# Second token blocks of a mixture of experts put behind a branch on every engine, and a new spread of the weight splits

## Chip, cores and metric

The kernel runs on one core of one Trainium2 chip. The metric is the device time of one execution in microseconds (us). The engines are TensorE (PE; its weight loads are PEld), VectorE (DVE), ScalarE (ACT), GpSimd (POOL) and SyncE (SP), which issues most transfers.

## The reference

One layer over 2048 tokens of width 1024: adaLN-modulated RMSNorm, a combined projection, softmax attention and retention, an output projection with a gated residual, and then a hierarchical mixture of experts. The change lies in the last part alone. Each token goes to 2 of 32 experts, so that an expert has 128 tokens on average, and some have more:

```
def expert_block(args):
    x_blk, e = args
    return (jax.nn.silu(x_blk @ w_gate[e]) * (x_blk @ w_up[e])) @ w_down[e]
```

The weights of an expert are 1024x512 (gate), 1024x512 (up) and 512x1024 (down) in float32. The result of a token is the weighted sum over its two experts, times a gate (gt2), added to the residual stream, and a final RMSNorm follows.

## The kernel before

The expert part is the function moe_static, run under a manual schedule: each engine executes its instructions in the order in which the code writes them. One pass of its loop over s is called a stage here; there are 31 of them, and the last expert is written out behind the loop.

The first 128 tokens of an expert are its first block (b = 0), tokens 129 to 256 its second block (b = 1). An expert of over 128 tokens is called heavy here, the others light. More than 256 tokens are handled by moe_more behind the loop.

Stage s does the gate and up products of expert s (gu, 24 matmuls of 512 columns each), the down product of expert d = s - 1 (down, twice 12 matmuls), and gathers, transposes and splits the tokens of expert s + 1 (gather, xT). Every float32 operand is split into a high part (a copy on ScalarE) and a low part (a subtraction on VectorE), and a product is three passes over the parts.

The weights of an expert come as 12 tiles of 128x1024 (wraw), loaded by SP into 9 buffers. advance(k) splits the next k tiles into whi (17 buffers, line 1535) and wlo (15 buffers, line 1536). The tuple AD says how many tiles are split at each of ten places of a stage, 12 in all: adv(0) behind gu(s, 0), adv(1) behind gu(s, 1), adv(2) behind act(s, 0), adv(3) behind xT(s + 1, 0), adv(4) behind act(s, 1), adv(5) to adv(8) around the two halves of down, adv(9) at the end. The split of a tile into a reused wlo buffer has to wait until TensorE has used the old tile, in the second block's product too.

The matmuls of the second block (gu_part, down_part) and its gather and scatter are issued by more: it loads the expert's token count into a register of the engine and branches on it. All else of the second block is done for all 32 experts, with zeros where there are no tokens: the eight transposes and two splits of xT(e, 1); the two folds of act(e, 1) (line 1606 on ScalarE, line 1607 on VectorE; a fold adds the upper 64 rows onto the lower), its SiLU and its product; the four transposes and the split of hT(e, 1); the two folds of evac_part; and its two multiplications by gt2 on GpSimd (line 1630). TR is a pair of PSUM tiles (tr) that all transposes share, so a transpose has to wait until the one before is split.

A branch under the framework has a second arm: where the body is skipped, the engine waits until its own earlier instructions have ended and then counts its semaphore up by what the body would have. That wait is called a join here.

Of the kernel before, what the change touches and what calls it, by code (L numbers as in the profile page):

```python
# [2 lines left out]

# [1 line left out]

# [6 lines left out]
F32 = mybir.dt.float32  # L12
# [3 lines left out]
AF = mybir.ActivationFunctionType  # L16
ALU = mybir.AluOpType
# [4 lines left out]
P = 128  # L22
D = 1024
KD = D // P
L = 2048
# [30 lines left out]
WA = 8  # L56
EA, EB, FIN = 3, 1, (4, 10, NT)
A0, A1, A2 = 6, 2, 4
AD = (3, 5, 0, 0, 0, 0, 0, 2, 2, 0)
XT = 2  # L60
PC = (4, 2, 4, 2, 2, 4, 4, 4, 4, 2)
PS = (4, 2, 2, 0, 0, 0, 0, 0, 0, 0, 2, 2, 2, 0, 2, 0, 2, 0)
# [70 lines left out]
class Build:  # L133
# [1374 lines left out]
    def moe_static(self, p, ps):  # L1508
        nc, tc, a = self.nc, self.tc, self.a
# [3 lines left out]
        Y = [ps.tile([P, 512], F32, name=f"Y{n}") for n in range(2)]  # L1513
        TR = [ps.tile([P, 4, P], F32, name=f"tr{i}") for i in range(2)]
        XG = [p.tile([P, D], F32, name=f"xg{b}", bufs=1) for b in range(2)]
        W, XT, SG, HT = {}, {}, {}, {}
        loads = self.moe_loads
        raws = self.moe_raws
        order = self.moe_order
# [8 lines left out]
        def advance(k):  # L1528

            for n in range(split_at[0], min(split_at[0] + k, len(order))):  # L1530
                raw = raws.pop(0)
                e, i = order[n]
                hi = p.tile([P, 1024], F32R, name="whi", bufs=WBH)
                lo = p.tile([P, 1024], F32R, name="wlo", bufs=WBL)
                nc.scalar.copy(hi, raw)  # L1535
                nc.vector.tensor_sub(lo, raw, hi)  # L1536
                W[e, i] = hi, lo
                load(1)
                split_at[0] = n + 1
# [6 lines left out]
        def gather(e):  # L1546
            nc.gpsimd.indirect_dma_start(
                out=XG[0], out_offset=None, in_=self.h2_d,
                in_offset=bass.IndirectOffsetOnAxis(ap=self.slots[:, 2 * e, 0:1], axis=0), bounds_check=L - 1, oob_is_err=False)

        def gather_part(e, b):
# [2 lines left out]
                out=XG[1][at], out_offset=None, in_=self.h2_d,  # L1554
                in_offset=bass.IndirectOffsetOnAxis(ap=self.slots[at, 2 * e + 1, 0:1], axis=0), bounds_check=L - 1, oob_is_err=False)

        def xT(e, b):
            x = p.tile([P, KD, 2, P], F32R, name="xT", bufs=2)
            cols = XG[b].rearrange("t (i p k) -> t i k p", p=P, k=2)
            for half in range(2):  # L1560
                for i in range(4):
                    nc.tensor.transpose(TR[half][:, i, :], cols[:, 2 * half + i // 2, i % 2, :], self.ident)
            for half in range(2):
                s_ = slice(4 * half, 4 * half + 4)
                split(x[:, s_], TR[half], b)
            XT[e, b] = x

        def split(out, t, b):

            hi, lo = out[:, :, 0, :], out[:, :, 1, :]  # L1570
            if b:
                hi, lo = (o.rearrange("p k (n h) -> p k h n", h=2) for o in (hi, lo))
                t = t.rearrange("p k (h n) -> p k h n", h=2)
            nc.scalar.copy(hi, t)  # L1574
            nc.vector.tensor_sub(lo, t, hi)

        def product(out, l, e, m, cols, K, rows):

# [7 lines left out]
        def gu(e, m):  # L1586
            product(GU[:, m, :], XT[e, 0], e, m, slice(0, 512), KD, 1)
# [5 lines left out]
        def act(e, b):  # L1593
            G = (GU, GB)[b]
            sg = p.tile([P, DE], F32, name="sg", bufs=2)
            if b:
                up = p.tile([P, DE], F32, name="up", bufs=1)
                fold(e, G[:, 0, :], 0, sg)
                fold(e, G[:, 1, :], 1, up)
            nc.scalar.activation(sg, sg if b else G[:, 0, :], AF.Silu)  # L1600
            nc.vector.scalar_tensor_tensor(sg, sg, W1[:, e:e + 1] if b else self.slots[:, 2 * e, 1:2].bitcast(F32), up if b else G[:, 1, :], op0=ALU.mult, op1=ALU.mult)
            SG[e, b] = sg

        def fold(e, src, n, out):

            nc.scalar.activation(LOW[n][0:64], src[64:128], AF.Copy, scale=self.few[64:128, e:e + 1])
            nc.vector.tensor_add(out, src, LOW[n])

        def hT(e, b):
            sg = SG.pop((e, b))  # L1610
            h = p.tile([P, 4, 2, P], F32R, name="hT", bufs=2)
            for i in range(4):
                nc.tensor.transpose(TR[b][:, i, :], sg[:, i * P:(i + 1) * P], self.ident)
            split(h, TR[b], b)
            HT[e, b] = h

        def down(e, n):
            product(Y[n], HT[e, 0], e, 2, slice(n * 512, (n + 1) * 512), 4, 1)
# [6 lines left out]
            nc.vector.tensor_mul(y[:, n, :], Y[n], self.gt2[:, n * 512:(n + 1) * 512])  # L1625

        def evac_part(e, y):
            for n in range(2):
                fold(e, Y[n], n, y[:, n, :])
                nc.gpsimd.tensor_mul(y[:, n, :], y[:, n, :], self.gt2[:, n * 512:(n + 1) * 512])  # L1630

        def y_tile():
            return p.tile([P, 2, 512], F32, name="y", bufs=YB)
# [6 lines left out]
        def scatter(e, b, y):  # L1640
            at = slice(0, 64 * b + 64)
            nc.gpsimd.indirect_dma_start(
                out=self.acc_d, out_offset=bass.IndirectOffsetOnAxis(ap=S1[at, e:e + 1], axis=0),
                in_=y[at].rearrange("p n f -> p (n f)"), in_offset=None, compute_op=ALU.add, bounds_check=L - 1, oob_is_err=False)

        def more(eng, e, f, *args):

            n = eng.value_load(self.cnt[0:1, e:e + 1], min_val=0, max_val=L)
            with tc.If(n > P):
                with tc.If(n <= P + 64) as few:  # L1650
                    f(e, 0, *args)
                with few.Else():
                    f(e, 1, *args)
# [9 lines left out]
        LOW = [p.tile([P, 512], F32, name=f"low{n}", bufs=1) for n in range(2)]  # L1663
# [18 lines left out]
        W1 = p.tile([P, NE], F32, name="W1", bufs=1)  # L1682
        S1 = p.tile([P, NE], I32, name="S1", bufs=1)
        t = p.tile([P, 2, NE], F32, name="pick", tag="sg", bufs=2)
# [62 lines left out]
        def last_add(b, y):  # L1747
            nc.gpsimd.tensor_add(fin[NT + b], fin[NT + b], y.rearrange("p n f -> p (n f)"))
# [6 lines left out]
        def adv(i):  # L1755
            if s < NE - 2 or i < 7:
                advance(AD[i] if s else max(0, min(AD[i], sum(AD[:i + 1]) - A2)))

# [7 lines left out]
        def down_more(d):  # L1766
            more(nc.tensor, d, down_part)
            y = y_tile()
            evac_part(d, y)
            return y  # L1770

        for s in range(NE - 1):
            d = s - 1
            gu(s, 0)
            adv(0)
            if s == 1 and HE:
                for b in range(2):
                    hT(0, b)
            gu(s, 1)
            adv(1)  # L1780
            act(s, 0)
            adv(2)
            if s == NE - 2:
                advance(EB)
            else:
                xT(s + 1, 0)
                gather(s + 2)
            adv(3)
            more(nc.tensor, s, gu_part)
            act(s, 1)  # L1790
            adv(4)
            if d >= 0:
                y = y_tile()
                down(d, 0)
                evac(0, y)
            adv(5)
            if s < NE - 2:
                xT(s + 1, 1)
            if s + 2 < NE:
                more(nc.gpsimd, s + 2, gather_part)  # L1800
            adv(6)
            if d >= 0:
                down(d, 1)
                evac(1, y)
                scatter_all(d, y)
                adv(7)
                y = down_more(d)
                adv(8)
                more(nc.gpsimd, d, scatter, y)
            else:  # L1810
                adv(7)
                adv(8)
            if s or not HE:
                hT(s, 0)
                hT(s, 1)
            adv(9)
            if s == NE - 2:
                advance(EA)
                fin["g"] = p.tile([P, D], F32, name="whi", bufs=WBH)
                nc.sync.dma_start(fin["g"], self.bcast(a["final_norm_g"], D))  # L1820
            if s == 1:
                t = p.tile([1, 3, NE], F32, name="blocks", tag="sg", bufs=2)
                nc.sync.dma_start(t[:, 0, :], a["riota"][0:1, 36:68])
                self.more_blocks(p, t[:, 0, :], t[:, 1, :], ("sg", "up"))
                nc.vector.reduce_sum(t[:, 2, 0:1], t[:, 1, :], axis=AX.X)
                nc.vector.tensor_copy(self.cnt[:, NE:], t[:, 2, 0:1])

        e = NE - 1
        scatter_all(e - 1, down_all(e - 1))
        more(nc.gpsimd, e - 1, scatter, down_more(e - 1))  # L1830
        for b in range(2):
            xT(e, b)
        advance(12 - EA - EB)
# [17 lines left out]
        final_rsqrt(ss[1], len(parts[1]))  # L1851
        y1 = down_more(e)
        last_add(0, y0)
        last_add(1, y1)
        final_scale(ss[1], parts[1])
        for i in (2, 3):
            final_squares(ss[i], parts[i])
# [178 lines left out]
```

## Time and profile before

| | us |
|---|---|
| median of 3 runs | 2525.8 |
| lowest and highest | 2525.15 and 2531.02 |
| profiled execution | 2530.7 |
| span of its instructions | 2528.7 |

The profile is of one execution, 4.9 us above the median. Its span runs from the first to the last instruction; 2.0 us lie around it. The expert part takes about the last 925 us of the span.

### The profile page before, as it was taken

Reading aid. Unit: us, or ns where it says so; the run is one execution under the profiler, and the core shown is the slowest. Engines: PE = TensorE matmul, PEld = TensorE weight load, DVE = VectorE, ACT = ScalarE, POOL = GpSimd, SP = SyncE. Lnnn points to the kernel's source line nnn. Section 1 sums busy time; section 2 is a strip of 40 time slices with the busy share of each in tenths; the row PEclk is TensorE's granted clock in tenths of the full one; section 3 lists DMA queues with packets and bytes.
Section 4 is the critical chain, followed back from the end, with each engine's and each line's share of the span. In section 5 each row is a group of like instructions: output and inputs, shape, how many; then the busy total and the mean of one; then the engine's idle time right before and its main releaser. Section 6 shows DMA issues by size and latency. Waiting matters only on the chain. (4 is left out here: it accounts for less than half of the span.)

```text
span 2528.7 us, 44704 instructions
## 1 busy us (share of the span) xinstructions
PE 2323.4 (92%) x15854; PEld 1951.3 (77%) x15854; DVE 2040.1 (81%) x3777; ACT 1614.7 (64%) x2459; POOL 1089.4 (43%) x1125
## 2 busy tenths in 40 slices
PE   7899999999999999999999998599998898989982
PEld 3788888887988888888987786477887777778761
DVE  6655555567999999999968887689989979897897
ACT  3533333336999999999953433567767767665664
POOL 2644444433666666666644443123323223232322
PEclk8999999998999999999999998799999999999996
DMA  7344444446111122230065531678878887887886
GB/s 264 101 113 116 116 119 114 121 124 177 35 52 51 43 62 66 61 85 22 23 236 180 176 120 66 197 241 281 281 255 287 293 271 252 275 297 237 251 269 275
DMA packets 208993, 417.65 MB, mean 165 GB/s; under 512 B 49466, under 2 KB 100962, under 8 KB 207538
## 3 DMA queue, kind: packets, MB, share of 16 engines
q1 hardware_dynamic: 173346, 363.00, 42.9%
q0 software_dynamic: 26656, 51.04, 8.8%
q8 instruction: 152, 2.49, 0.4%
q10 hardware_dynamic: 8736, 0.27, 0.2%
q14 instruction: 103, 0.84, 0.1%
HBM read 336.97 MB, written 86.23 MB: 167 GB/s over the span
## 5 line engine op out<-in xcount | busy, mean ns | idle before, releaser
L1536 DVE TENSOR_TENSOR wlo<-wraw,whi 128x1024 fp32r<-128x1024 f32 x384 | 488.1, 1326 | 58.8 <-issue 52.9
L950 POOL TENSOR_TENSOR pl<-p,ph 128x512 f16<-128x512 f32 (+1 forms) x320 | 341.7, 1068 | 239.3 <-DVE pl L950 127.5
L1535 ACT CAST whi<-wraw 128x1024 fp32r<-128x1024 f32 x384 | 377.1, 1055 | 19.3 <-DMA wraw<-in_moe_w_gate 10.9
L899 DVE TENSOR_REDUCE mx<-sm 128x1 f32<-128x512 f32 x512 | 336.6, 682 | 25.3 <-PE sm L898 21.3
L934 ACT ACTIVATE p<-st,cexp 128x1024 f32<-128x1024 f32 (+1 forms) x320 | 328.9, 1028 | 19.0 <-PE st L932 11.0
L1583 PE MATMUL gu<-whi,xT 128*128 128x512 f32 x1024 | 325.7, 394 | 0.0
L943 ACT CAST ph<-p 128x1024 f16<-128x1024 f32 (+1 forms) x320 | 308.0, 962 | 7.2
L931 PE MATMUL st<-qhh,KHL 128*128 128x256 f32 x1152 | 299.5, 290 | 0.5 <-ACT p L934 0.5
L932 PE MATMUL st<-qlm,KO 65*128 65x256 f32 x1152 | 294.1, 286 | 0.0
L434 PE MATMUL pp<-whi,hT_hi 128*128 128x512 f32 (+1 forms) x688 | 263.3, 383 | 5.4 <-ACT v L625 3.3
L434 PE MATMUL pp<-whi,hT_lo 128*128 128x512 f32 (+1 forms) x688 | 256.4, 373 | 2.7 <-POOL hT_lo L413 1.5
L434 PE MATMUL pp<-wlo,hT_hi 128*128 128x512 f32 (+1 forms) x688 | 255.5, 371 | 0.9 <-DVE wlo L388 0.9
L950 DVE TENSOR_TENSOR pl<-p,ph 128x514 f16<-128x514 f32 (+1 forms) x320 | 247.8, 774 | 8.8 <-ACT ph L943 7.4
L963 PE MATMUL o<-vx,ph 128*128 128x129 f16 x2304 | 247.4, 223 | 4.4 <-ACT ob L971 4.4
L898 PE MATMUL sm<-KHL,qhh 128*128 128x512 f32 x512 | 233.7, 460 | 10.2 <-DVE mx L899 9.2
L965 PE MATMUL o<-vx,pl 128*128 128x65 f16 x2304 | 235.9, 193 | 0.0
L963 PEld LDWEIGHTS <-ph 128*128 128x128 f16 x2304 | 201.2, 97 | 41.0 <-issue 35.5
L1583 PE MATMUL Y<-whi,hT 128*128 128x512 f32 x624 | 227.5, 420 | 5.4 <-ACT hT L1574 1.9
L932 PEld LDWEIGHTS st<-qlm,KO 65*128 65x128 f32 x1152 | 222.1, 193 | 10.6
L931 PEld LDWEIGHTS st<-qhh,KHL 128*128 128x128 f32 x1152 | 223.6, 194 | 1.0 <-ACT p L934 0.7
L1583 PEld LDWEIGHTS gu<-whi,xT 128*128 128x128 f32 x1024 | 193.2, 189 | 39.5
L965 PEld LDWEIGHTS <-pl 128*128 128x128 f16 x2304 | 205.9, 99 | 4.8 <-DVE pl L950 2.9
(356 smaller groups left out, 5144.9 us busy)
## 6 DMA issues: line engine op xcount, KB each, us to landing
wraw<-in_moe_w_gate SPq DMA_DIRECT2D x128, 512.0 KB, 3.9
wraw<-in_moe_w_up SPq DMA_DIRECT2D x128, 512.0 KB, 5.1
wraw<-in_moe_w_down SPq DMA_DIRECT2D x128, 512.0 KB, 7.1
wa<-in_w_ada SPq DMA_DIRECT2D x64, 256.0 KB, 2.9
wa<-in_w_ada SPq DMA_DIRECT2D x8, 1024.0 KB, 8.8
wraw<-in_w_in SPq DMA_DIRECT2D x32, 256.0 KB, 2.9
xt<-in_x SPq DMA_DIRECT2D x16, 512.0 KB, 4.7
qh_d<-qt SPq DMA_DIRECT2D x64, 128.0 KB, 2.5
```

Source lines behind the costliest of these rows:

```text
L434: ins = nc.tensor.matmul(out[:, :n], l[:, k, :], r[:, k, c0:c0 + n], start=(k == 0 and i == 0), stop=(k == KD - 1 and i == 2))
L899: nc.vector.reduce_max(mx[u][:, j, n:n + 1], sm, axis=AX.X)
L931: nc.tensor.matmul(st[:, n, :], khl[h // 4][:, kt * P:(kt + 1) * P], qhh[:, h % 4, :], start=True, stop=False)
L932: nc.tensor.matmul(st[:, n, :], ko[h // 4][:, kt * P:(kt + 1) * P], qlm[:, h % 4, :], start=False, stop=True)
L934: nc.scalar.activation(p32[:, :len(ks)], st[:, :len(ks)], AF.Exp, bias=cexp)
L943: nc.scalar.copy(cols(PH[i], 0, n), cols(P32[i], 0, n))
L950: eng.tensor_sub(cols(PL[i], a, b), cols(P32[i], a, b), cols(PH[i], a, b))
L963: nc.tensor.matmul(o[:, j, 0:2 * HD + 1], ph[:, n, s_], vx[:, kt, g, :], start=(kt == 0 and j == 0), stop=False, skip_group_check=True)
L965: nc.tensor.matmul(o[:, j, 0:HD + 1], pl[:, n, s_], vx[:, kt, g, 0:HD + 1], start=False, stop=(kt == NTT - 1), skip_group_check=True)
L1535: nc.scalar.copy(hi, raw)
L1536: nc.vector.tensor_sub(lo, raw, hi)
L1583: nc.tensor.matmul(out, l[:, k].rearrange("p a n -> p (a n)")[:, 0::2] if a_ is None else l[:, k, a_, :], w[r], start=(k == 0 and i == 0), ...
```

## The change

Two helpers are new: count loads an expert's token count once for each engine and keeps the register, and when opens a branch on "over 128 tokens" for second blocks and does nothing for first blocks. All work of second blocks now stands in such a branch of its engine: four on TensorE for each expert (two of them are those of more), five on ScalarE, five on VectorE. On GpSimd the two multiplications by gt2 move into the branch of the scatter (put_part). Folds come in pairs, first both on ScalarE, then both on VectorE. For the last expert the multiplications and the add of the second block stand behind a branch as well. AD changes from (3, 5, 0, 0, 0, 0, 0, 2, 2, 0) to (3, 3, 0, 1, 1, 0, 0, 2, 2, 0).

```diff
-AD = (3, 5, 0, 0, 0, 0, 0, 2, 2, 0)
+AD = (3, 3, 0, 1, 1, 0, 0, 2, 2, 0)
...
+        def count(eng, e):
+
+            if (eng, e) not in counts:
+                counts[eng, e] = eng.value_load(self.cnt[0:1, e:e + 1], min_val=0, max_val=L)
+            return counts[eng, e]
+
+        def when(eng, e, b):
+
+            return tc.If(count(eng, e) > P) if b else nullcontext()
...
+            with when(nc.tensor, e, b):
+                for half in range(2):
+                    for i in range(4):
+                        nc.tensor.transpose(TR[half][:, i, :], cols[:, 2 * half + i // 2, i % 2, :], self.ident)
+            split(e, [(x[:, 4 * half:4 * half + 4], TR[half]) for half in range(2)], b)
...
+            with when(nc.scalar, e, b):
+                for hi, lo, t in views:
+                    nc.scalar.copy(hi, t)
+            with when(nc.vector, e, b):
+                for hi, lo, t in views:
+                    nc.vector.tensor_sub(lo, t, hi)
...
+        def fold(e, pairs):
+
+            with when(nc.scalar, e, 1):
+                for n, (src, out) in enumerate(pairs):
+                    nc.scalar.activation(LOW[n][0:64], src[64:128], AF.Copy, scale=self.few[64:128, e:e + 1])
+            with when(nc.vector, e, 1):
+                for n, (src, out) in enumerate(pairs):
+                    nc.vector.tensor_add(out, src, LOW[n])
...
+            with when(nc.tensor, e, b):
+                for i in range(4):
+                    nc.tensor.transpose(TR[b][:, i, :], sg[:, i * P:(i + 1) * P], self.ident)
+            split(e, [(h, TR[b])], b)
...
+        def put_part(e, b, y):
             for n in range(2):
-                fold(e, Y[n], n, y[:, n, :])
                 nc.gpsimd.tensor_mul(y[:, n, :], y[:, n, :], self.gt2[:, n * 512:(n + 1) * 512])
+            scatter(e, b, y)
...
-        last_add(1, y1)
+        with when(nc.gpsimd, e, 1):
+            for n in range(2):
+                nc.gpsimd.tensor_mul(y1[:, n, :], y1[:, n, :], self.gt2[:, n * 512:(n + 1) * 512])
+            last_add(1, y1)
```

VectorE in the middle of a stage, before: two weight splits of adv(1), the product of act(s, 0), the split of xT(s + 1, 0), the folds and the product of act(s, 1), a result of down, and the split of xT(s + 1, 1). In brackets stand the engines and transfers that a row waits for.

```order
L1536 TENSOR_TENSOR wlo<-wraw,whi 128x1024 [waits DMAHW4_49,Activation_49]
L1536 TENSOR_TENSOR wlo<-wraw,whi 128x1024 [waits DVE_49,DMAHW5_49,PE_49,Activation_49]
L1601 SCALAR_TENSOR_TENSOR sg<-sg,slots,gu 128x512 [waits Activation_49]
L1575 TENSOR_TENSOR xT<-tr_21974,xT 128x4x128 [waits Activation_49]
L1575 TENSOR_TENSOR xT<-tr_21975,xT 128x4x128 [waits Activation_49]
L1607 TENSOR_TENSOR sg<-gb,low_22022 128x512 [waits Activation_49]
L1649 UNCONDITIONAL_BRANCH
L1607 TENSOR_TENSOR up<-gb,low_22023 128x512 [waits Activation_49]
L1601 SCALAR_TENSOR_TENSOR sg<-sg,W_22109,up 128x512 [waits DVE_49,Activation_49]
L1625 TENSOR_TENSOR y<-Y_21972,gt_6130 128x512 [waits DMASW7_49,PE_49]
L1575 TENSOR_TENSOR xT<-tr_21974,xT 128x4x2x64 [waits Activation_49]
L1575 TENSOR_TENSOR xT<-tr_21975,xT 128x4x2x64 [waits Activation_49]
```

Nothing here is conditional; the second row waits for PE, and all that follows stands behind it. The same place in the change, from the product of act(s, 0) on, with the branch of the folds:

```order
L1618 SCALAR_TENSOR_TENSOR sg<-sg,slots,gu 128x512 [waits DVE_49,Activation_49]
L1674 UNCONDITIONAL_BRANCH
L1591 TENSOR_TENSOR xT<-tr_21974,xT 128x4x128 [waits Activation_49]
L1623 UNCONDITIONAL_BRANCH
L1591 TENSOR_TENSOR xT<-tr_21975,xT 128x4x128 [waits Activation_49]
L1536 TENSOR_TENSOR wlo<-wraw,whi 128x1024 [waits DMAHW4_49,Activation_49]
L1626 COMPARE_AND_BRANCH
L1628 TENSOR_TENSOR sg<-gb,low_22022 128x512 [waits PE_49,Activation_49,Pool_49]
L1628 TENSOR_TENSOR up<-gb,low_22023 128x512 [waits Pool_49]
L1626 UNCONDITIONAL_BRANCH
L1626 UNCONDITIONAL_BRANCH [waits DVE_49]
...
L1536 TENSOR_TENSOR wlo<-wraw,whi 128x1024 [waits DVE_49,DMAHW5_49,PE_49,Activation_49]
```

The split that waits for PE stood ahead of the product of act(s, 0) and the split of xT; it now stands behind both and behind the folds. The folds have a branch, whose last row is the join.

TensorE before: the transposes of xT(s + 1, 1) between the two halves of down, and, behind the join of down_part, those of hT(s, 0) and hT(s, 1).

```order
L1562 MATMUL tr_21974<-ident,xg_21977 128x128 [waits DMASW6_49,DVE_49]
L1562 MATMUL tr_21974<-ident,xg_21977 128x128 x3
L1562 MATMUL tr_21975<-ident,xg_21977 128x128 [waits DVE_49]
L1562 MATMUL tr_21975<-ident,xg_21977 128x128 x3
...
L1649 UNCONDITIONAL_BRANCH [waits PE_49]
L1613 MATMUL tr_21974<-ident,sg 128x128 [waits DVE_49]
L1613 MATMUL tr_21974<-ident,sg 128x128 x3
L1613 MATMUL tr_21975<-ident,sg 128x128 [waits DVE_49]
L1613 MATMUL tr_21975<-ident,sg 128x128 x3
```

Both groups are done for every expert, and each waits for VectorE's split of the one before. TensorE in the change, the same places (the second piece begins with hT's branch):

```order
L1570 COMPARE_AND_BRANCH
L1573 MATMUL tr_21974<-ident,xg_21977 128x128 [waits DMASW2_49,DMASW4_49,DMASW0_49,DMASW6_49,DVE_49,Pool_49]
L1573 MATMUL tr_21974<-ident,xg_21977 128x128 x3
L1573 MATMUL tr_21975<-ident,xg_21977 128x128 [waits DVE_49]
L1573 MATMUL tr_21975<-ident,xg_21977 128x128 x3
L1570 UNCONDITIONAL_BRANCH
L1570 UNCONDITIONAL_BRANCH [waits PE_49]
...
L1633 COMPARE_AND_BRANCH
L1635 MATMUL tr_21975<-ident,sg 128x128 [waits DVE_49,Activation_49]
L1635 MATMUL tr_21975<-ident,sg 128x128 x3
L1633 UNCONDITIONAL_BRANCH
L1633 UNCONDITIONAL_BRANCH [waits PE_49]
```

Both groups of transposes of the second block now lie between a branch and a join that waits for PE itself. The bodies' waits now name more transfers than before, and other engines.

## Rows read from the trace of the kernel before

**Rows 1.** The page's busy time, share of the span and instructions of each engine.
```profile
PE 2323.4 (92%) x15854; PEld 1951.3 (77%) x15854; DVE 2040.1 (81%) x3777; ACT 1614.7 (64%) x2459; POOL 1089.4 (43%) x1125
```

**Rows 2.** Windows: busy us (instructions) of PE, PEld, DVE, ACT, POOL; clock; DMA.
```profile
1862.10:1892.50 30.40, 30.39 (x142) 24.94 (x141) 26.12 (x29) 18.66 (x25) 9.69 (x5) 1.00 0.81 269
1941.40:1966.50 25.10, 20.86 (x94) 16.76 (x92) 23.77 (x27) 18.73 (x26) 7.18 (x4) 0.93 0.86 288
2211.80:2234.40 22.60, 21.05 (x104) 16.94 (x102) 21.74 (x25) 18.52 (x25) 8.62 (x5) 1.00 0.90 300
1642.60:2436.90 794.30, 742.99 (x3426) 606.51 (x3424) 695.81 (x761) 539.96 (x698) 246.08 (x140) 0.97 0.82 269
```

**Rows 3.** Line 1600, SiLU of first blocks: one per expert, first and last start.
```profile
L1600 ACT ACTIVATE sg<-gu x32: 577/596/611, 1623.3 to 2473.8; 128x512 f32<-128x512 f32 x32
```

**Rows 4.** Tile gb, products of second blocks: duration min/median/max, first and last start.
```profile
L1583 PE MATMUL gb<-whi,xT x224: 389/395/491, 1642.5 to 2387.0; 128*128 128x512 f32 x112
L1583 PE MATMUL gb<-wlo,xT x208: 389/394/396, 1642.9 to 2387.2; 128*128 128x512 f32 x104
```

**Rows 5.** Timeline of TensorE's weight loads near a skipped second block: start, us.
```profile
1916.01 0.19 PEld L1583 LDWEIGHTS gu<-wlo,xT 128*128 128x128 f32 x1
1916.69 0.19 PEld L1583 LDWEIGHTS gu<-wlo,xT 128*128 128x128 f32 x1
1917.14 1.15 PEld L1562 LDWEIGHTS tr<-ident,xg 128*128 128x128 f32 x8
1918.60 0.19 PEld L1583 LDWEIGHTS Y<-whi,hT 128*128 128x128 f32 x1 [0.31 <-issue]
```

**Rows 6.** Waits from 1640 to 2440 us: total us, times, longest.
```profile
DVE wlo L1536 <- issue: 52.9, 12, 6.3
PEld tr L1562 <- DVE xT L1575: 52.0, 29, 4.4
...
SPq L1504 <- DVE wlo L1536: 645.7, 349, 9.2
```

**Rows 7.** Timeline of VectorE and GpSimd, 1850 to 1858 us.
```profile
1850.46 2.34 DVE L1536 TENSOR_TENSOR wlo<-wraw,whi 128x1024 fp32r<-128x1024 f32 x2
1853.92 4.17 DVE L1536 TENSOR_TENSOR wlo<-wraw,whi 128x1024 fp32r<-128x1024 f32 x2
...
1853.48 3.53 POOL L1630 TENSOR_TENSOR y<-y,gt 128x512 f32<-128x512 f32 x2 [0.36 <-DVE y L1607]
```

**Rows 8.** Timeline of VectorE, 1859 to 1876 us.
```profile
1859.22 8.02 DVE L1536 TENSOR_TENSOR wlo<-wraw,whi 128x1024 fp32r<-128x1024 f32 x7
1870.10 1.23 DVE L1536 TENSOR_TENSOR wlo<-wraw,whi 128x1024 fp32r<-128x1024 f32 x1 [2.87 <-issue]
1871.90 1.28 DVE L1575 TENSOR_TENSOR xT<-tr,xT 128x512 fp32r<-128x512 f32 x2
1874.54 0.69 DVE L1607 TENSOR_TENSOR up<-gb,low 128x512 f32<-128x512 f32 x1 [0.75 <-ACT low L1606]
```

**Rows 9.** Line 1649, the branch in more; line 1915, a register load of each engine.
```profile
L1649 POOLq COMPARE_BRANCH  x64: 34/45/53, 1600.6 to 2521.5; - x64
L1649 PEldq COMPARE_BRANCH  x64: 65/218/363, 1617.6 to 2483.6; - x64
...
L1915 DVEq TENSOR_LOAD <-cnt x1: 541/541/541, 2517.3 to 2517.3; - x1
```

**Rows 10.** Timeline of VectorE and GpSimd in the tail.
```profile
2481.45 4.86 DVE L1721 SCALAR_TENSOR_TENSOR whi<-whi,ss 128x1024 f32<-128x1024 f32 x4
2492.21 7.40 DVE L1721 SCALAR_TENSOR_TENSOR wlo<-wlo,ss,whi 128x1024 f32<-128x1024 f32 x3
...
2491.78 3.48 POOL L1630 TENSOR_TENSOR y<-y,gt 128x512 f32<-128x512 f32 x2 [20.63 <-DVE y L1607]
2498.50 3.32 POOL L1748 TENSOR_TENSOR whi<-whi,y 128x1024 f32<-128x1024 f32 x1
```

**Rows 11.** DMA from 1940 to 1992 us: GB/s in 40 slices.
```profile
GB/s 303 372 321 347 397 410 413 425 419 274 16 0 110 290 151 221 290 350 384 252 337 321 265 366 403 419 416 419 425 271 3 60 243 221 195 268 318 394 306 274
```

More of the change, by code (lines that the diff above doesn't have):

```diff
@@ L1 @@
 import math
-from contextlib import ExitStack
+from contextlib import ExitStack, nullcontext
 import numpy as np
@@ L1515, in moe_static @@
         XG = [p.tile([P, D], F32, name=f"xg{b}", bufs=1) for b in range(2)]
-        W, XT, SG, HT = {}, {}, {}, {}
+        W, XT, SG, HT, counts = {}, {}, {}, {}, {}
         loads = self.moe_loads
@@ L1559, in xT, with split @@
             cols = XG[b].rearrange("t (i p k) -> t i k p", p=P, k=2)
[L1560 to L1565, printed above, removed]
-            XT[e, b] = x
[L1568 to L1575, printed above, removed]
+            with when(nc.tensor, e, b):
[3 more added lines that the diff above has]
+            split(e, [(x[:, 4 * half:4 * half + 4], TR[half]) for half in range(2)], b)
+            XT[e, b] = x
+        def split(e, pairs, b):
+            views = []
+            for out, t in pairs:
+                hi, lo = out[:, :, 0, :], out[:, :, 1, :]
+                if b:
+                    hi, lo = (o.rearrange("p k (n h) -> p k h n", h=2) for o in (hi, lo))
+                    t = t.rearrange("p k (h n) -> p k h n", h=2)
+                views.append((hi, lo, t))
+            with when(nc.scalar, e, b):
[4 more added lines that the diff above has]
+                    nc.vector.tensor_sub(lo, t, hi)
         def product(out, l, e, m, cols, K, rows):
@@ L1597, in act @@
                 up = p.tile([P, DE], F32, name="up", bufs=1)
[L1598 to L1601, printed above, removed]
-            SG[e, b] = sg
-        def fold(e, src, n, out):
-            nc.scalar.activation(LOW[n][0:64], src[64:128], AF.Copy, scale=self.few[64:128, e:e + 1])
-            nc.vector.tensor_add(out, src, LOW[n])
+                fold(e, ((G[:, 0, :], sg), (G[:, 1, :], up)))
+            with when(nc.scalar, e, b):
+                nc.scalar.activation(sg, sg if b else G[:, 0, :], AF.Silu)
+            with when(nc.vector, e, b):
+                nc.vector.scalar_tensor_tensor(sg, sg, W1[:, e:e + 1] if b else self.slots[:, 2 * e, 1:2].bitcast(F32), up if b else G[:, 1, :], op0=ALU.mult, op1=ALU.mult)
+            SG[e, b] = sg
+        def fold(e, pairs):
[5 more added lines that the diff above has]
+                    nc.vector.tensor_add(out, src, LOW[n])
         def hT(e, b):
@@ L1611, in hT @@
             h = p.tile([P, 4, 2, P], F32R, name="hT", bufs=2)
-            for i in range(4):
-                nc.tensor.transpose(TR[b][:, i, :], sg[:, i * P:(i + 1) * P], self.ident)
-            split(h, TR[b], b)
+            with when(nc.tensor, e, b):
+                for i in range(4):
+                    nc.tensor.transpose(TR[b][:, i, :], sg[:, i * P:(i + 1) * P], self.ident)
+            split(e, [(h, TR[b])], b)
             HT[e, b] = h
@@ L1627, in evac_part @@
         def evac_part(e, y):
+            fold(e, [(Y[n], y[:, n, :]) for n in range(2)])
+        def put_part(e, b, y):
             for n in range(2):
-                fold(e, Y[n], n, y[:, n, :])
                 nc.gpsimd.tensor_mul(y[:, n, :], y[:, n, :], self.gt2[:, n * 512:(n + 1) * 512])
+            scatter(e, b, y)
         def y_tile():
@@ L1646, in more @@
         def more(eng, e, f, *args):
-            n = eng.value_load(self.cnt[0:1, e:e + 1], min_val=0, max_val=L)
+            n = count(eng, e)
             with tc.If(n > P):
@@ L1808, in moe_static @@
                 adv(8)
-                more(nc.gpsimd, d, scatter, y)
+                more(nc.gpsimd, d, put_part, y)
             else:
@@ L1829, in moe_static @@
         scatter_all(e - 1, down_all(e - 1))
-        more(nc.gpsimd, e - 1, scatter, down_more(e - 1))
+        more(nc.gpsimd, e - 1, put_part, down_more(e - 1))
         for b in range(2):
```

## The prediction

> **What bounds the kernel now.** The page first: TensorE is busy 92% of the span and VectorE 81% [rows 1]. These are averages over all phases, and a busy TensorE includes time in which a matmul's modelled end only bridges a gap, so I went to the expert part. Its first SiLU starts at 1623.3 us and that of expert 31 at 2473.8 us [rows 3]: the 31 stages take 850.5 us. The high part of gb's weights, with 208 matmuls on the low part at 16 for each heavy expert, gives 13 heavy experts; the 16 matmuls more on the other side [rows 4] are one expert of over 192 tokens, which takes three passes instead of two. The last product on gb is at 2387 us, so expert 31 is light, and of the 31 stages 18 belong to light experts.
>
> What a stage needs of TensorE: two loads of low weights three matmuls apart lie 0.68 us apart, so a matmul costs 0.227 us; eight transposes cost 1.15 us with the last one's own length, 1.0 us without; behind a skipped second block, TensorE idles 0.31 us, which I take as the price of a join [rows 5]. For four transposes I take half of eight, 0.5 us. A light stage is then 72 x 0.227 + 2 x 1.0 + 2 x 0.5 + 2 x 0.31 = 19.9 us, where it follows a light one.
>
> Then three windows. The stage from 1862.1 us (expert and the one before it both heavy) has 72 + 32 + 16 matmuls, 27.2 + 3.0 = 30.2 us of work in 30.4 us: TensorE bounds it. The light stage from 1941.4 us has 19.9 us of work in 25.1 us, with VectorE busy 23.8 us; the one from 2211.8 us takes 22.6 us, VectorE 21.7 us [rows 2]. So light stages are VectorE's and heavy ones TensorE's. The waits agree: the weight loads of transposes wait 52.0 us for VectorE's xT splits, SP waits 645.7 us for wlo before it can reload a buffer, and not the other way round [rows 6].
>
> Over all 31 stages, TensorE's work before is 31 x (16.3 + 3.0) = 598 us, plus 432 x 0.23 = 99 us on gb, plus second down products of 12 x 16 + 24 = 216 matmuls or 50 us, plus 36 joins or 11 us: 758 us. The remaining 92 us are idle time, and only from them and from the removed transposes can the change take.
>
> **What is removed.** On TensorE 12 transposes for each light expert, 1.5 us, 18 times: 27 us.
>
> On VectorE, for each light expert: the xT split 1.28 us, a fold 0.69 us and one like it, with the 0.75 us wait between them [rows 8]; one product, two more folds and one more split of the same 512 columns, at 0.65 us each 2.6 us. That is 6.0 us. GpSimd's two multiplications go too; while they ran for 3.5 us, two weight splits took 4.17 us instead of 2.34 us [rows 7], another 1.8 us. What VectorE still does in a light stage: 12 weight splits at 8.02 / 7 = 1.15 us [rows 8], 13.8 us, the first block's xT split 1.28 us and four operations at 0.65 us: 17.7 us. With the 7.8 us removed it is 25.5 us; the light stage from 1941.4 us lasts 25.1 us. ScalarE is busy 18.7 us in it [rows 2] and loses as much; it isn't late.
>
> **What is added.** Two more joins on TensorE for each light expert, 36 x 0.31 = 11 us. Five joins each on VectorE and ScalarE, which the trace doesn't show. Below, the compare itself is 0.045 us on GpSimd; above, a register load fully exposed, 0.54 us [rows 9], plus TensorE's 0.31 us, 0.85 us. I take 0.3 us, since a join of TensorE is the same sequence: 1.5 us a stage. Behind the joining instruction stand the next splits, and the loads wait for these. VectorE's light stage becomes 19.2 us, TensorE's 72 x 0.227 + 1.0 + 0.5 + 4 x 0.31 = 19.1 us. Heavy experts pay only a compare; it lies beside queued work there, since TensorE bounds the stage, and without that cover five compares at 0.2 us would cost 1 us, 13 us over all. The register loads are one per expert and engine; the queued split of 1.15 us covers them.
>
> [...]
>
> **What is moved.** The split that waits for PE. In the heavy stage from 1862.1 us it starts at 1870.10 us after 2.87 us of idle, and the xT split behind it at 1871.90 us [rows 8], although its transposes had long been done. In all, VectorE stands 52.9 us in 12 such waits [rows 6]. With AD changed, the product, the xT split and one weight split run in that time, and TR is free when TensorE comes to xT(s + 1, 1). VectorE's stall goes behind the folds, which wait for the same product anyway; no load is later than before, since the number of splits ahead of the next stage is the same. The transfers issued are the same as well, save GpSimd's order: a skipped scatter no longer has 3.5 us of multiplications ahead of it.
>
> **Sum.** Work changes by -27 + 11 = -16 us. Of the 92 us of idle I leave 40 us: 1.5 us in each light stage (27 us), because two engines now need the same 19 us; 0.7 us in each heavy one (9 us); 4 us at the last stages, where final loads mix in. That is -52 us. In the tail expert 31 is light. VectorE's scaling takes 7.40 us for three tiles while GpSimd works, against 4.86 us for four before that; of GpSimd's four operations 3.48 us and 3.32 us go [rows 10], which at the same rate frees 4 us; the folds and the split on the way free 2 us more. Together -16 - 52 - 6 = -74 us: 2530.7 to 2457 us for the profiled execution, which lies 4.9 us above the median, and 2452 us from the median of 2525.8 us.
>
> **Rivals.** *The loads become the bound of light stages.* The quickest light stage moved 300 GB/s for 22.6 us, 6.8 MB [rows 2]; in 19.2 us that is 353 GB/s. For it: no stage shown holds more than 300 GB/s. Against it: slices of 1.3 us reach 425 GB/s, and the mean is held down by slices near 0 [rows 11], when no buffer is free. If 300 GB/s is the most, light stages stay at 22.6 us, idle is 18 x 3.5 + 13 = 76 us, and the gain 16 + 16 + 6 = 38 us: 2488 us.
>
> *The idle time stays.* If TensorE's waits for VectorE only change their place, to the transposes of hT or the next expert's weights, only work and tail are gained, 22 us: 2504 us. Against it: light stages equal VectorE's sum to within 0.5 us.
>
> *A skip costs far more than TensorE's 0.31 us on VectorE, and the kernel gets slower.* With p for a join, a light stage is 17.7 + 5p. The gain is nil where idle reaches 92 + 22 = 114 us, 5.6 us in a light stage, which is p = 1.4 us. At p = 2 us idle is 18 x 8.6 + 13 = 168 us: 54 us slower, 2580 us. Against it: TensorE's 0.31 us, the compares, and a register load of only 0.54 us [rows 5, 9]; for it: VectorE has no row of a skipped branch. [...]
>
> **How the numbers follow.** About 0.3% is what a measurement of this kernel can tell from no change. Chances: the forecast 0.62, loads 0.20, idle stays 0.10, slower 0.07; 0.01 for no change. The range runs from 2426 us (16 us of idle left, tail 8 us: 16 + 76 + 8 = 100 us) to 2492 us, the loads' case with 4 us of joins that show on top. Faster 0.91, same 0.02, slower 0.07.
>
> **What would show it.** Light stages of 20 to 21.5 us; VectorE at some 18 us of work in them; TensorE's waits for xT splits near 10 us; heavy stages shortened by at most 1 us; no multiplication of GpSimd in light stages; the wait of VectorE for wlo now behind the folds. It would be wrong if idle before an instruction behind a join on VectorE or ScalarE is over 1 us, if light stages hold at 22.6 us with ScalarE waiting for wraw, or if TensorE waits as long for hT as it did for xT.

## The result and the profile after

| | before | after |
|---|---|---|
| median, us | 2525.5 (4 runs) | 2434.2 (4 runs) |
| lowest and highest, us | 2525.1 and 2531.0 | 2433.7 and 2437.2 |
| profiled execution, us | 2530.7 | 2433.9 |

The ratio is 0.9633, with a 95% interval of 0.962 to 0.9646: 91 us less. The forecast was 74 us less, 2452 us, with a range from 2426 to 2492 us.

The page's line of busy time, which answers to [rows 1]:

```profile
PE 2269.8 (93%) x15626; PEld 1907.3 (78%) x15626; DVE 1912.0 (79%) x3625; ACT 1524.9 (63%) x2307; POOL 1002.1 (41%) x1086
```

Shares say little again, so the stages come next. SiLU of first blocks now stands on line 1616; its row answers to [rows 3].

```profile
L1616 ACT ACTIVATE sg<-gu x32: 577/598/602, 1615.1 to 2383.3; 128x512 f32<-128x512 f32 x32
```

The 31 stages take 768.2 us instead of 850.5 us: 82.3 us of the gain lie here. From the last mark to the end of the span it is 48.5 us instead of 54.9 us, 6.4 us less, and from the last matmul ahead of the expert part to the first mark 37.0 us instead of 39.0 us, 2.0 us less. Together that is 90.7 us, the gain of the medians. The two profiled spans differ by 6 us more; those lie in phases ahead of the experts whose instructions are the same, and the profiled execution of before was itself 4.9 us above its median.

Windows answer to [rows 2]: a heavy stage behind a heavy one, three light stages that follow a light one, the whole loop from the second mark to the last, and the tail. The columns are those of [rows 2].

```profile
1844.00:1873.90 29.90, 29.75 (x138) 24.43 (x138) 22.49 (x25) 17.52 (x23) 7.36 (x5) 1.00 0.81 268
1896.50:1916.00 19.50, 18.75 (x87) 14.89 (x86) 17.78 (x19) 13.99 (x17) 3.36 (x2) 1.00 0.99 334
1916.00:1935.40 19.40, 18.65 (x86) 14.79 (x86) 17.61 (x19) 14.20 (x17) 3.36 (x2) 1.00 1.03 387
2143.40:2162.80 19.40, 18.65 (x86) 14.79 (x86) 17.68 (x19) 14.11 (x17) 5.10 (x3) 1.00 1.00 348
1632.70:2348.00 715.30, 700.73 (x3232) 572.47 (x3230) 588.84 (x632) 462.99 (x566) 171.03 (x108) 1.00 0.88 300
2383.30:2431.80 48.50, 10.15 (x28) 7.08 (x28) 34.35 (x70) 17.23 (x31) 4.15 (x2) 0.57 0.72 292
```

The light stage shrank from 25.1 us to 19.4 us, with VectorE's work down from 23.8 us to 17.6 or 17.8 us and all transfers together at up to 387 GB/s (335 GB/s of that are SP's queue, which loads the weights). The heavy stage went from 30.4 us to 29.9 us. By the marks, the 16 light stages inside the loop (all but the first and the last of the 31) went from 407.5 us to 341.2 us and the 13 heavy ones from 386.8 us to 374.1 us. The granted clock of a light stage is 1.00, where it was 0.93 in the stalled light stage of before. In that one it was 0.50 for 3.4 us from 1949.0 us, behind a wait of TensorE of 4.0 us for an xT split, and matmuls started 0.43 us apart instead of 0.23 us. Over the 31 stages it was 0.50 for 51.2 us before, in ten stretches, and for 13.6 us after, in three.

What is waited for from 1640 to 2350 us: waiting engine, tile and line, whom for, total us, times, longest. It answers to [rows 6].

```profile
DVE sg L1628 <- ACT low L1625: 71.0, 12, 8.9
...
DVE wlo L1536 <- ACT whi L1535: 5.9, 18, 0.4
...
DVE mth L1907 <- DMA blocks<-in_riota: 5.3, 1, 5.3
...
DVE wlo L1536 <- DVEq L1617: 4.4, 7, 0.6
ACT whi L1535 <- DMA wraw<-in_moe_w_gate: 4.1, 5, 1.8
...
DVE wlo L1536 <- DVEq L1589: 3.4, 16, 0.2
DVE wlo L1536 <- DVEq L1626: 3.4, 16, 0.2
```

TensorE's wait for xT splits, 52.0 us before, is gone. VectorE's long stall stands behind the folds of heavy experts now, 71.0 us in 12 waits, where TensorE is the bound. DVEq is VectorE's own sequencer: these rows are its joins, 0.2 us each, and 0.6 us where two follow each other. ScalarE waits only 4.1 us for arriving weights in the row shown, and 4.7 us with a smaller one.

The light stage from 1896.5 us on VectorE (timeline; idle before and its end in brackets):

```profile
1897.50 0.73 DVE L1618 SCALAR_TENSOR_TENSOR sg<-sg,slots,gu 128x512 f32<-128x512 f32 x1
1898.16 1.27 DVE L1591 TENSOR_TENSOR xT<-tr,xT 128x512 fp32r<-128x512 f32 x2
1899.36 1.21 DVE L1536 TENSOR_TENSOR wlo<-wraw,whi 128x1024 fp32r<-128x1024 f32 x1
1901.20 1.23 DVE L1536 TENSOR_TENSOR wlo<-wraw,whi 128x1024 fp32r<-128x1024 f32 x1 [0.63 <-PE Y L1599]
1902.34 0.68 DVE L1647 TENSOR_TENSOR y<-Y,gt 128x512 f32<-128x512 f32 x1
1903.68 0.69 DVE L1647 TENSOR_TENSOR y<-Y,gt 128x512 f32<-128x512 f32 x1 [0.66 <-PE Y L1599]
...
1906.85 2.36 DVE L1536 TENSOR_TENSOR wlo<-wraw,whi 128x1024 fp32r<-128x1024 f32 x2 [0.21 <-DVEq L1626]
1909.13 0.68 DVE L1591 TENSOR_TENSOR hT<-tr,hT 128x512 fp32r<-128x512 f32 x1
1910.02 6.90 DVE L1536 TENSOR_TENSOR wlo<-wraw,whi 128x1024 fp32r<-128x1024 f32 x6 [0.21 <-DVEq L1589]
```

And TensorE's weight loads in the same stage, which answer to [rows 5]:

```profile
1897.51 0.19 PEld L1599 LDWEIGHTS Y<-whi,hT 128*128 128x128 f32 x1 [0.31 <-ACT sg L1616]
...
1900.64 0.19 PEld L1599 LDWEIGHTS Y<-whi,hT 128*128 128x128 f32 x1 [0.54 <-issue]
...
1903.91 0.42 PEld L1635 LDWEIGHTS tr<-ident,sg 128*128 128x128 f32 x4 [0.69 <-issue]
1904.68 0.19 PEld L1599 LDWEIGHTS gu<-whi,xT 128*128 128x128 f32 x1 [0.36 <-issue]
```

These four breaks are the four joins, and nothing else breaks the stream. A weight load starts 0.22 or 0.23 us ahead of its matmul in this stage, and 0.03 us ahead right behind a join, so the breaks of the loads are not those of the matmuls. From one matmul's start to the next's it is 0.227 us elsewhere (0.11 to 0.12 us between transposes); at the four joins this step is longer by 0.31, 0.31, 0.46 and 0.31 us, and behind all but the third the next step by 0.08 us more, 1.6 us in all. With 72 x 0.227 + 1.0 + 0.5 us that is 19.4 us, the whole stage. TensorE is its bound now. VectorE has little to spare: the 0.63 us are two joins in a row (the split behind them needs no Y, and the same gap is put down to DVEq elsewhere), and of the 0.66 us before the second result of down 0.21 us are a join, so 0.45 us are a wait for TensorE.

VectorE in the tail, which answers to [rows 10]:

```profile
2401.35 3.67 DVE L1746 SCALAR_TENSOR_TENSOR wlo<-wlo,ss,whi 128x1024 f32<-128x1024 f32 x3 [0.24 <-DVEq L1626]
2404.94 3.67 DVE L1746 SCALAR_TENSOR_TENSOR wraw<-wraw,ss,whi 128x1024 f32<-128x1024 f32 x3
```

Three tiles take 3.67 us, where they took 7.40 us while GpSimd worked.

### The profile page after: what moved, and what is told of

The parts are those of the page before. It is cut to its first block, busy times and chain, and to the rows that moved or that the text cites. A ratio compares the mean times of both kernels' runs of the same rounds, so it can differ in the third digit from the quotient of the medians.

```text
span 2431.8 us, 44974 instructions
## 1 busy us (share of the span) xinstructions
PE 2269.8 (93%) x15626; PEld 1907.3 (78%) x15626; DVE 1912.0 (79%) x3625; ACT 1524.9 (63%) x2307; POOL 1002.1 (41%) x1086
## 5 line engine op out<-in xcount | busy, mean ns | idle before, releaser
L1536 DVE TENSOR_TENSOR wlo<-wraw,whi 128x1024 fp32r<-128x1024 f32 x384 | 460.0, 1246 | 27.5 <-ACT whi L1535 6.8
L1599 PE MATMUL Y<-whi,hT 128*128 128x512 f32 x624 | 216.8, 403 | 9.6 <-DVEq L1589 2.5
```

The lines of the kernel that those rows point to most:

```text
L1599: nc.tensor.matmul(out, l[:, k].rearrange("p a n -> p (a n)")[:, 0::2] if a_ is None else l[:, k, a_, :], w[r], start=(k == 0 and i == 0), ...
```

## The experiments

Each kernel was timed against the kernel before on the same chip, and what it differs from the changed kernel is worked out from the ratios: (its ratio - 0.9633) x 2525.5 us. The two intervals together make such a difference uncertain by 5 to 7 us. Stage n runs from the mark of expert n, its first SiLU, to the next one.

### The new spread of splits (AD)

e1_old_ad is the changed kernel with the old spread, e2_ad_alone the kernel before with the new one.

```diff
-AD = (3, 3, 0, 1, 1, 0, 0, 2, 2, 0)
+AD = (3, 5, 0, 0, 0, 0, 0, 2, 2, 0)
```

> All branches, the old AD. My theory (light stages were bound by VectorE's second-block work, so the branches carry the gain): VectorE now has slack, so a split that waits for PE ahead of the first block's product costs little; 2438 to 2452 us. Rival (the split at the head of VectorE's queue was the main cause): the gain shrinks to half or less, 2475 us or more.

> The kernel before with the new AD alone, no branch added. My theory: VectorE still needs 25.5 us in a light stage, so only the 2.87 us waits in heavy stages are turned to use, 10 to 20 us in all: 2505 to 2516 us. Rival (the head of VectorE's queue): 40 us or more, 2485 us or less.

e1_old_ad took 2448.1 us, 0.9683 (0.9666 to 0.9699): 13 us slower than the changed kernel. e2_ad_alone took 2517.3 us, 0.996 (0.9946 to 0.9973): 10 us faster than before. So the spread is worth 10 to 13 us with the branches or without. The first lies in the range of its theory; the second misses it by 1 us, and its rival by far. In e1_old_ad, VectorE and TensorE's loads in the light stage from 2089.3 us:

```profile
2085.01 8.03 DVE L1536 TENSOR_TENSOR wlo<-wraw,whi 128x1024 fp32r<-128x1024 f32 x7
2092.96 0.74 DVE L1618 SCALAR_TENSOR_TENSOR sg<-sg,slots,gu 128x512 f32<-128x512 f32 x1
2093.62 1.28 DVE L1591 TENSOR_TENSOR xT<-tr,xT 128x512 fp32r<-128x512 f32 x2
```

```profile
2094.37 1.13 PEld L1573 LDWEIGHTS tr<-ident,xg 128*128 128x128 f32 x8 [1.45 <-issue]
```

Seven splits in a row stand ahead of the product, so the xT split begins 4.3 us behind the mark, and TensorE's transposes of the next expert's second block, which need TR, wait 1.45 us. The stage takes 21.9 us; the same one of the changed kernel takes 20.0 us, and no load of transposes waits there. The 31 stages take 777.1 us, 8.9 us more, and such a wait of 1.0 to 1.4 us stands in each of the seven light stages ahead of a heavy one, 8.4 us together. That is the end of the chain which the prediction gave for the move (a late xT split holds TR), but not its head: VectorE waits ahead of a weight split for TensorE in only two places, 9.7 us, where it was 52.9 us in 12 before, and the seven splits stand in a row without a gap. Nor are the heavy stages longer with the old spread: the 13 take 372.3 us, the changed kernel's 374.1 us. In e2_ad_alone it is the other way round: its heavy stages take 377.8 us instead of 386.8 us, its light ones no less than before. ScalarE waits 45.8 us for weights in e1_old_ad, but VectorE waits for ScalarE's copies no longer than in the changed kernel (5.2 and 5.9 us).

### TensorE without its new branches

In e3_pe_all the transposes of second blocks are done for every expert; in light ones they transpose old data that nobody reads.

```diff
-            return tc.If(count(eng, e) > P) if b else nullcontext()
+            return tc.If(count(eng, e) > P) if b and eng is not nc.tensor else nullcontext()
```

> As the change, but TensorE does the second blocks' transposes for all experts; their results are used by heavy experts only. My theory: 12 transposes for 2 joins, 1.5 - 0.6 = 0.9 us in each light stage, 16 us, and a few us of waits for TR: 2448 to 2458 us. Rival (TensorE's own transposes and their waits carry the gain): 2475 us or more.

2444.0 us, 0.9667 (0.9651 to 0.9683): 9 us slower than the changed kernel, where my theory had 14 us or more. The four light stages 11 to 14 take 20.1 us each, where the changed kernel takes 19.4 or 19.5 us in the first three and 20.0 us in stage 14, ahead of a heavy expert. In the first three, twelve transposes of 1.5 us less two joins of 0.39 us make 0.7 us; in stage 14, four transposes of 0.5 us less one join make 0.1 us: both as measured. Light stages thus follow TensorE's own work to a tenth of a microsecond, which is what a bound does.

### VectorE and ScalarE without their branches

In e4_pe_pool both do all second blocks' work (in light experts on old data that nobody reads); TensorE's and GpSimd's branches and the new spread stay.

```diff
-            return tc.If(count(eng, e) > P) if b else nullcontext()
+            return tc.If(count(eng, e) > P) if b and eng is not nc.vector and eng is not nc.scalar else nullcontext()
```

> As the change, but VectorE and ScalarE do the second blocks' work for all experts; for light ones on old data that nothing reads. My theory: VectorE's light stage is 17.7 + 6.0 = 23.7 us, 4.3 us above the 19.4 us of the change, 18 times: some 77 us lost, 2500 to 2515 us. Rival (TensorE's part carries the gain): 2455 us or less.

2481.5 us, 0.9821 (0.9805 to 0.9838): 47 us slower than the changed kernel and 45 us faster than before. Both theories missed. Two light stages in a row, 12 and 13:

```profile
1927.50:1948.50 21.00, 18.68 (x86) 14.77 (x85) 20.71 (x26) 18.50 (x24) 3.36 (x2) 1.00 0.96 333
1948.50:1972.50 24.00, 20.15 (x86) 15.87 (x86) 23.72 (x28) 18.50 (x24) 6.40 (x3) 0.93 0.95 329
```

VectorE is busy for nearly all of both, so it is the bound again, but with 22.2 us a stage on the mean (11 weight splits in the first, 13 in the second), not 23.7 us. The work that its branches remove is therefore 22.2 - 17.7 = 4.5 us a light stage, not 6.0 us: the durations that I added up overlap by some 0.07 us from one instruction to the next, and 0.75 us of them was a wait. The stage is 22.5 us on the mean against 19.4 us, and all 16 light ones together 41 us longer; the last stage and the tail add 4 us.

### ScalarE's copies without branches

In e5_act_all, ScalarE's halves of splits and folds are done for every expert, on old data in light ones; SiLU keeps its branch. Both places, in split and in fold (there with 1 for b), get this edit:

```diff
-            with when(nc.scalar, e, b):
+            with nullcontext():
```

> As the change, but ScalarE does the second blocks' copies and folds (not their SiLU) for all experts; for light ones on old data that nothing reads. My theory: ScalarE goes from 14 to some 18.4 us in a light stage, still under TensorE's 19.4 us: 2434 to 2442 us. Rival (ScalarE's share was needed too, since its folds wait for products at the head of its queue): 2450 us or more.

2436.1 us, 0.9642 (0.9623 to 0.9661): no difference that can be told. ScalarE is busy 17.0 us instead of 14.0 us in the light stage, which stays at 19.4 us:

```profile
1896.50:1916.00 19.50, 18.75 (x86) 14.90 (x85) 17.62 (x19) 17.03 (x24) 5.53 (x3) 1.00 1.00 331
```

So e4_pe_pool's loss was VectorE's (ScalarE's SiLU of 0.6 us, which it also did for all experts, was not tried by itself), and what ScalarE's copies lose is worth nothing here.

### GpSimd's two multiplications

e6_pool_alone is the kernel before with nothing but GpSimd's multiplications moved into the branch of the scatter.

```diff
+        def put_part(e, b, y):
+            for n in range(2):
                 nc.gpsimd.tensor_mul(y[:, n, :], y[:, n, :], self.gt2[:, n * 512:(n + 1) * 512])
+            scatter(e, b, y)
...
-                more(nc.gpsimd, d, scatter, y)
+                more(nc.gpsimd, d, put_part, y)
...
```

> The kernel before, with only GpSimd's two multiplications moved into the branch of the scatter. My theory: VectorE's splits lose the 1.8 us that they spend beside the multiplications in each of 18 light stages, and VectorE bounds these: 32 us, 2488 to 2500 us. Rival (the contention falls into time in which VectorE would wait anyway): 2518 us or more.

2513.7 us, 0.9945 (0.993 to 0.9961): 14 us faster than before, between the two theories. To see the same price from the other side, e9_muls gives the changed kernel the multiplications back, and those alone.

```diff
...
+                with tc.If(count(nc.gpsimd, d) <= P):
+                    for n in range(2):
+                        nc.gpsimd.tensor_mul(ones, ones, self.gt2[:, n * 512:n * 512 + 480])
                 more(nc.gpsimd, d, put_part, y)
```

> The changed kernel, in which GpSimd multiplies 128x480 elements twice in the place of the removed multiplications (on a tile of its own that nobody reads), for light experts alone; heavy experts keep theirs. It measures by itself what these two multiplications cost where everything else of the second blocks is skipped. Theory: the multiplications hold up VectorE's weight splits by the sum read from the trace, here with 15/16 of the elements some 1.5 us a light stage. VectorE has 17.7 us of work and some 1.1 us of joins there, which makes 20.3 us against TensorE's 19.4 us: 0.9 us in each of 16 light stages of the loop, 14 us, 2444 to 2454 us by the median, with VectorE's busy time in a light stage near 19.2 us. Rival one: VectorE's lag is caught up by the buffers of weights in heavy stages and next to nothing shows, 2433 to 2440 us. Rival two: GpSimd itself gets late with the gathers and scatters that stand behind the multiplications, and the light stages grow by the 3.3 us of the multiplications, 2470 us or more.

2452.6 us, 0.9687 (0.9664 to 0.971): 14 us slower than the changed kernel, and 16.3 us more in the stages. Both rivals are out. VectorE in the light stage from 1945.2 us, which takes 21.1 us, and its window:

```profile
1954.81 2.35 DVE L1536 TENSOR_TENSOR wlo<-wraw,whi 128x1024 fp32r<-128x1024 f32 x2
1957.37 4.66 DVE L1536 TENSOR_TENSOR wlo<-wraw,whi 128x1024 fp32r<-128x1024 f32 x2 [0.21 <-DVEq L1626]
```

```profile
1945.20:1966.30 21.10, 18.77 (x86) 14.79 (x86) 19.89 (x19) 14.25 (x17) 8.62 (x5) 1.00 1.02 359
2066.20:2092.60 26.40, 24.15 (x102) 18.98 (x102) 22.32 (x24) 15.30 (x19) 9.09 (x6) 0.94 0.96 312
```

Two splits take 4.66 us instead of 2.35 us beside GpSimd, as in [rows 7], and VectorE's work is 19.9 us instead of 17.7 us. How the multiplications hold up the splits, no run shows. The time is not lost only where it arises: the 8 light stages that follow a light one (4, 11 to 14, 19, 22 and 23), and in which GpSimd multiplies, grow by 7 us together, and the 8 that follow a heavy one by 10 us. Neither is spread evenly. Stages 4, 11, 19 and 22 grow by 0.1 us each: VectorE is held up there as well, but ends them two weight splits further behind than in the changed kernel. The light stages behind them (12 to 14 and 23) grow by 1.5 to 1.7 us each; of those that follow a heavy one, 16, 18, 21 and 29 grow by 1.5 to 3.7 us, and 3, 7, 10 and 27, behind two heavy ones, by 0.1 us. The second window is stage 18. In the heavy stage ahead of it, VectorE has its wait for the fold first and the splits beside GpSimd afterwards, so that the wait absorbs none of it:

```profile
2049.28 0.69 DVE L1628 TENSOR_TENSOR sg<-gb,low 128x512 f32<-128x512 f32 x1 [5.44 <-PE Y L1599]
...
2056.99 4.64 DVE L1536 TENSOR_TENSOR wlo<-wraw,whi 128x1024 fp32r<-128x1024 f32 x2 [0.21 <-ACT hT L1588]
```

At the light stage's first mark VectorE is two weight splits further behind than in the changed kernel; it does 14 of them in the stage instead of 12, which takes 26.4 us instead of 22.7 us. My sum of 14 us came out, but not as I had it: not 0.9 us in each of 16 light stages, but 1.5 to 3.7 us in eight of them and next to nothing in the other eight. That the two sums agree is partly luck.

### The price of a join

e7_joins puts one branch more behind each weight split of stages 1 to 30, with a write of one element inside that only heavy experts do.

```diff
...
+                if stage[0] is not None:
+                    with when(nc.vector, stage[0], 1):
+                        nc.vector.memset(tiny, 0.0)
...
```

> As the change, with one more branch on VectorE behind each of 12 weight splits of a stage, around a write of one number; light stages skip it, heavy ones run it. It measures a join on VectorE. My theory (p about 0.2 to 0.3 us): VectorE's light stage grows by 2.4 to 3.6 us from some 18.7 us, past TensorE's 19.4 us by 2 to 3 us, 18 times: 2465 to 2495 us. Rival (a skip costs 1 us or more): 2600 us or more. Rival (a skip is hidden in VectorE's queue): 2434 to 2440 us.

2485.5 us, 0.9828 (0.9811 to 0.9844): 49 us slower than the changed kernel. VectorE's waits from 1640 to 2400 us (first row: the new join), and its timeline at the begin of a light stage:

```profile
DVE wlo L1538 <- DVEq L1540: 23.2, 99, 0.6
DVE wlo L1538 <- ACT whi L1537: 12.4, 31, 1.2
```

```profile
1910.06 1.22 DVE L1538 TENSOR_TENSOR wlo<-wraw,whi 128x1024 fp32r<-128x1024 f32 x1 [0.22 <-DVEq L1540]
1911.51 1.22 DVE L1538 TENSOR_TENSOR wlo<-wraw,whi 128x1024 fp32r<-128x1024 f32 x1 [0.22 <-DVEq L1540]
1912.96 0.75 DVE L1623 SCALAR_TENSOR_TENSOR sg<-sg,slots,gu 128x512 f32<-128x512 f32 x1 [0.22 <-DVEq L1540]
```

With a join behind each, splits start 1.45 us apart; without, six of them take 6.90 us, 1.15 us each, as the row at 1910.02 us of the changed kernel shows. So a join costs VectorE 0.30 us: a gap of 0.22 us, and the 0.07 us by which two splits otherwise overlap. Twelve of them are 3.6 us a stage. The light stages 11 to 14 take 22.8 us on the mean instead of 19.6 us, 3.2 us more, as VectorE had some 0.45 us to spare. The prediction's 0.3 us a join was right, and 1 us is out by far.

### A version with a row loaded earlier

In the changed kernel, stage 1 contains a wait of 5.3 us of VectorE for a row of constants (riota), loaded on SP's queue behind weights. e8_early_row loads it ahead of the loop on ScalarE's queue.

```diff
+        blocks = p.tile([1, 3, NE], F32, name="blocks", bufs=1)
+        nc.scalar.dma_start(blocks[:, 0, :], a["riota"][0:1, 36:68])
...
-                t = p.tile([1, 3, NE], F32, name="blocks", tag="sg", bufs=2)
-                nc.sync.dma_start(t[:, 0, :], a["riota"][0:1, 36:68])
+                t = blocks
```

> As the change, with the row of numbers that stage 1 needs for its count of further blocks loaded ahead of the loop, in a tile of its own. VectorE waits 5.3 us for that transfer in stage 1, and TensorE has 4.4 us of idle in the stage after. If the one makes the other: 4 us faster than the change, 2428 to 2431 us. If the idle time is due to the weights: no change.

2431.8 us, 0.9624 (0.9611 to 0.9637). Stages 1 and 2, first of the changed kernel, then of this one:

```profile
1632.70:1661.90 29.20, 28.90 (x142) 24.23 (x141) 18.18 (x25) 17.03 (x22) 4.75 (x3) 1.00 0.69 234
1661.90:1693.60 31.70, 29.43 (x126) 23.66 (x125) 28.10 (x31) 17.48 (x22) 6.85 (x5) 0.95 0.84 255
```

```profile
1637.90:1665.10 27.20, 26.90 (x130) 22.36 (x129) 21.45 (x29) 17.03 (x22) 3.89 (x2) 1.00 0.73 250
1665.10:1695.10 30.00, 29.85 (x139) 24.55 (x139) 24.87 (x27) 17.53 (x23) 8.09 (x5) 1.00 0.83 271
```

The two stages take 57.2 us instead of 60.9 us, and the wait is gone. The time of the whole is 2 us less, the lowest of all kernels here, but the intervals do not tell it from the changed kernel; only the two stages speak for the first expectation.

## Why the prediction was right, and where its sizes were off

**The bound of a light stage: right.** VectorE set it at 25.1 us and was to fall to 17.7 us of work, TensorE to 19.1 us. Measured are 17.6 to 17.8 us and 19.4 us. TensorE's 0.3 us more are joins: three of the four cost 0.39 us and one 0.46 us instead of 0.31 us, which is the gap of the weight loads alone. With its joins VectorE was to need 19.2 us, a tie; the runs show TensorE as the bound.

**The removed work on VectorE: right only in its end.** I had 7.8 us in a light stage, 6.0 us of its own and 1.8 us from GpSimd. e4_pe_pool shows 4.5 us for the first. The second is 1.6 us as what is left of 23.8 - 17.7 us, and 2.2 us in e9_muls. Since I added up both what goes and what stays, and built the forecast on what stays, the error cost nothing. That 17.7 + 7.8 us came near the 25.1 us of the light stage was luck in part: VectorE was busy 23.8 us in it. ScalarE does not lose "as much" either, but 4.7 us, from 18.7 us to 14.0 us.

**Idle time left: the step that was mis-sized.** "Of the 92 us of idle I leave 40 us" is the term behind most of the 17 us between forecast and result. By the same sum of work, 742 us, the stages of 768.2 us leave 26 us, 14 us less. The 1.5 us that each light stage was to lose "because two engines now need the same 19 us" are not there: the stage is 19.4 us where TensorE's work and joins are 19.4 us. VectorE has 0.45 us to spare in it, and e9_muls shows that weight splits can fall behind into the next stage, which evens out what the two engines need. Of the 26 us, 9 us lie in the last of the stages, where TensorE is busy 26.3 of 35.2 us, and some 4 us in stages 1 and 2, which e8_early_row took away. The prediction also counted as idle what TensorE lost at its lower clock, of which it does not speak: 51.2 us of the stages before and 13.6 us after were at a granted clock of 0.50. Matmuls were 0.43 us apart in it instead of 0.23 us, so nearly half of such time is lost: of the 37.6 us between the two, 19 us at most by my estimate. The light stages of before with a stretch of it were the longest (28.0 us on the mean behind a heavy one, against 25.0 us without), but no run holds the clock fixed, so whether it made them longer or only followed their waits stays open. The tail's 6.4 us met its term of 6 us, and the 2.0 us ahead of the first mark were not in the sum.

**The joins: right.** On VectorE 0.30 us each by e7_joins (taken: 0.3 us), with a gap of 0.21 or 0.22 us; in the changed kernel no gap behind one exceeds 0.64 us in the stages, but for one of 1.01 us in the last of them. There the split starts 0.65 us after the second of two joins, elsewhere 0.27 us, so that some 0.4 us of the gap are another wait. Over 1 us was to refute the forecast. TensorE's stage has no break beside its four joins, and its work and these joins make up the whole 19.4 us, so the branches of other engines in its order cost it nothing that shows.

**The moved split: right in its price, only half in its place.** The wait moved behind the folds, 71.0 us in 12 waits, and TensorE's 52.0 us for xT splits are gone, of which I had left some 10 us. Either change by itself takes most of them: 15.8 us stay in e2_ad_alone, 8.7 us in e1_old_ad. The heavy stages became shorter by 12.7 / 13 = 1.0 us, the most that I had allowed, but the branches do that without the move (372.3 us in e1_old_ad). e1_old_ad and e2_ad_alone give the move 10 to 13 us: in heavy stages, as the prediction had it, in the kernel before, and mostly in light stages ahead of a heavy one in the changed kernel.

**Rivals.** *The loads* were refuted: the light stages inside the loop run at 320 to 387 GB/s, beyond the 300 GB/s of the quickest light stage before, as the short slices of [rows 11] had suggested, and ScalarE's wait for weights is 4.7 us. So buffers had held them back, not the transfers. The DMA share is 0.99 to 1.03 in the light windows shown, though, at 334 to 387 GB/s; whether the transfers have room left, no run shows. *The idle time stays* was refuted by the stages, *a skip costs far more* by e7_joins.

**What each part is worth.** Taken out of the changed kernel one by one, the spread costs 13 us, GpSimd's branch 14 us, TensorE's 9 us, and VectorE's with ScalarE's 47 us: 83 us, with 5 to 7 us of uncertainty in each, of the 91 us. Alone in the kernel before, the spread gave 10 us and GpSimd's branch 14 us, the same within that. VectorE's branch without ScalarE's was not tried.

## What to carry to other kernels

Work out for each engine what it still has to do in a stage, not what is taken from it: the larger of two such sums was the stage to within 0.3 us here, while the sum of removed durations was off by a third. Do not add idle time for two engines that need about the same, as long as buffers let one of them fall behind for a stage; and a saving in a stage with another bound may come back in the next. A branch that skips even a few microseconds of a bounding engine's work paid here, where a skip with its join cost 0.30 us on VectorE and 0.39 to 0.46 us on TensorE, and skipping GpSimd's two multiplications in each light stage gave VectorE time as well, worth 14 us of the kernel's.

## What the runs showed of the hardware

A join cost each engine its own price: a gap of 0.21 or 0.22 us on VectorE, some 0.63 us where two follow each other, and 0.39 to 0.46 us on TensorE. One core's transfers held 387 GB/s over a whole stage of 19.4 us, 1.26 times the most of any stage of before, 307 GB/s. VectorE's weight splits took 4.66 us for two instead of 2.35 us beside GpSimd's multiplications in e9_muls, although the two share no data in these instructions.
